# Key and value casts kept at their written places, and tile gaps that set moving and stationary addresses 416 bytes apart modulo 512

## The chip, the core and the metric

The kernel runs on one core of a Trainium2 chip. The metric is the time of one execution on the device in microseconds (us), lower is better. Beside it stands one execution taken by the hardware profiler; its records of engines, DMAs and waits are called the trace, and a summary of it is called the profile's page. PE is the matrix engine, PEld its weight loads, ACT, DVE and POOL are the scalar, vector and general engines, SP the engine that issues most DMAs.

## What is computed

One layer of an encoder for 256 positions of width 2048: several mixers side by side and an output projection, then cross attention to 256 memory rows, then a gated feed-forward part. Cut to the parts that the change touches:

```python
def cross_attention(h, mem_n, w_q, w_kv, w_o):          # 4 heads of 512
    q = (h @ w_q).reshape(bsz, seq, XA_HEADS, XA_HD)
    k, v = jnp.split(mem_n @ w_kv, 2, axis=-1)
...
    s = jnp.einsum('bshd,bmhd->bhsm', q, k).astype(jnp.float32) * XA_HD ** -0.5
    p = jax.nn.softmax(s, axis=-1).astype(v.dtype)
    o = jnp.einsum('bhsm,bmhd->bshd', p, v).reshape(bsz, seq, D_MODEL)
    return o @ w_o

def swiglu(h, w_gate_up, w_down):                       # inner width 5632
    gate, up = jnp.split(h @ w_gate_up, 2, axis=-1)
    return (jax.nn.silu(gate) * up) @ w_down
...
    x = x + mix @ w_out[l]
    x = x + cross_attention(rms_norm(x, norm_g[l, 1]), mem_n, w_xq[l], w_xkv[l], w_xo[l])
    x = x + swiglu(rms_norm(x, norm_g[l, 2]), w_gate_up[l], w_down[l])
```

## The kernel before, in words

**Precision.** Every large product is made from numbers split in a high part (rounded to the matrix engine's fast 4-byte type) and a low part (the rest). A tile of activations is 128 x 512: 256 columns of high parts and 256 of low parts. `mm` (L262 to L272) makes one 128 x 128 weight block's share of a product from two matmuls: the high weights `wh` with all 512 columns (L269), and the low weights `wl` with the 256 high columns (L270). The two together are called a pair here. The weights are the stationary operand, the activations the moving one. (`narrow` columns, L266 and L267, use three matmuls of 256 columns.) `gemm_rows` (L321 to L323) has them the other way round.

**Weights.** `Stream` reads all weights in the order of use. `_half` loads 2048 columns by SP's queue into one of three `raw` buffers and casts them, 1024 columns at a time, on ACT (`wh`, L89) and subtracts on DVE (`wl`, L90). Such a half feeds eight pairs. `wh` and `wl` have three buffers each, and a fourth while the pool `wx` is open (the mixers and the attention, up to nearly the end of `w_xo`).

**Stages, in the order of PE.** The keys and values of the memory (`w_xkv`), written to DRAM; the mixers (`w_in`); the output projection `out_proj` (`w_out`, 16 columns of 16 blocks); the attention (`w_xq` head by head, for each head the scores, softmax and values in `head`; then `w_xo`); `mlp` (`w_gate_up`, then `w_down`, 16 columns of 44 blocks: 8 tiles `act4` to `act11` and 36 tiles `f0` to `f35`). In `out_proj` the first four columns are made together, in three parts of the 16 blocks, because the mixers' results come late; each of the four columns has its own PSUM bank of the four in pool `psG`. The fifth column needs the first one's bank again. A finished bank is evacuated by `merge` (L274 to L278): ACT copies half of it (L276), DVE adds the other half (L178).

**Keys and values.** `load_kv`, a generator that runs beside the matmuls, brings the 16 key pieces and 16 value pieces back from DRAM. `fetch` (L580) issues a DMA on POOL's queue into one of five buffers `mr`. A key piece is cast on ACT (L186) and subtracted on DVE (L178, called by `split`), a value piece likewise (L194 and L178, called by `split2`); then the next piece is fetched.

**What sets the order.** Each engine runs its instructions in one fixed order. The Python program writes them in some order: `Background` polls the generators between matmuls, by planned costs. After that a scheduler of the framework orders each engine's instructions again by its own estimate of when they are ready, within their dependencies. In the kernel before, 16 of the 32 casts and subtractions of keys and values (those of heads 0 and 1) stand in ACT's and DVE's order in the first part of `out_proj`, far ahead of the place where the program writes them, which is among the first heads' query products. On ACT they stand between the casts of weights: four key casts, a value cast, a weight cast, two value casts, a weight cast, and so on, 16 in all, and 15 of them stand ahead of the copy (L276) that evacuates `out_proj`'s first column. The other 16 stand in four bursts of four among the products of heads 2 and 3.

**Addresses.** The tile pools give every tile one start address per partition. Those that matter here, modulo 512:

| tile | role | before | after |
|---|---|---|---|
| `act0` to `act23` | moving (stationary in `gemm_rows`) | 128 | 128 |
| `wh`, `wl` | stationary | 224 | 224 |
| `f0` to `f35` | moving, `w_down` | 224 | 128 |
| `oex0` to `oex3` | moving, `w_xo` | 224 | 128 |
| `kt` | moving, scores | 256 | 256 |
| `q` | stationary, scores | 256 | 352 |
| `pt` | moving, values | 224 | 128 |
| `vh`, `vl` | stationary, values | 256 | 224 |

Weight blocks are 512 bytes wide, so all blocks of a half have one place modulo 512, and so do the high and low halves of a moving tile.

Of the kernel before, what the change touches and what calls it, by code (L numbers as in the profile page):

```python
# [13 lines left out]
F32 = mybir.dt.float32  # L14
F32R = mybir.dt.float32r
# [7 lines left out]
P = 128  # L23
# [126 lines left out]
class Block:  # L150
# [42 lines left out]
    def split2(self, hi, lo, src):  # L193
        self.nc.scalar.copy(hi, src)  # L194
        self.tt(lo, src, hi.bitcast(F32), ALU.subtract)

    def sumsq(self, acc, src, first):
        if first:
            self.nc.scalar.activation(acc, src, AF.Square)
        else:  # L200
            s = self.tmp()
            self.nc.scalar.activation(s, src, AF.Square)
            self.tt(acc, acc, s, ALU.add)
# [343 lines left out]
    def attention(self):  # L547
        tc, nc, act, st = self.tc, self.nc, self.act, self.st
        with tc.tile_pool(name="atp", bufs=1) as atp, tc.tile_pool(name="kp", bufs=1) as kp, \
                tc.tile_pool(name="mp", bufs=5) as mp:  # L550
            oex = [atp.tile([P, 512], F32R, name=f"oex{i}") for i in range(4)]
            pt = [atp.tile([P, 512], F32R, name=f"pt{i}") for i in range(2)]
            qs = atp.tile([P, 2], F32, name="qs")
            o = act[0:8] + oex + act[8:12]
            slot = lambda name, n: kp.tile([P, 512], F32R, name=name, tag=name, bufs=n)
            kv = [([], [], []) for _ in range(4)]

            def ev_q(q, p):
                q.append(slot("q", 8))
                self.split(q[-1], self.merge(p))  # L560

            def scales():

                col = self.rstd_begin([[self.acc]], D)
                nc.vector.tensor_scalar(out=qs, in0=col, scalar1=512 ** -0.5, scalar2=None, op0=ALU.mult)
                yield

            heads = []

            def load_kv():  # L570

                todo = [(hd, what, i) for hd in range(4) for what in range(2) for i in range(4)]
                parts = []

                def fetch():
                    if len(parts) < len(todo):
                        hd, what, i = todo[len(parts)]
                        m = mp.tile([P, R], F32, name="mr", tag="mr")
                        o = (4 * hd + i) * R
                        nc.gpsimd.dma_start(m, (self.vd if what else self.kd)[:, o:o + R])  # L580
                        parts.append(m)

                for _ in range(5):
                    fetch()
                yield 4
                for n, (hd, what, i) in enumerate(todo):
                    while hd > len(heads) + 1:
                        yield
                    if what == 0:
                        kv[hd][0].append(slot("kt", 8))  # L590
                        self.split(kv[hd][0][-1], parts[n])
                    else:
                        if i % 2 == 0:
                            kv[hd][1].append(slot("vh", 4))
                            kv[hd][2].append(slot("vl", 4))
                        c = slice(i % 2 * R, i % 2 * R + R)
                        self.split2(kv[hd][1][-1][:, c], kv[hd][2][-1][:, c], parts[n])
                    fetch()
                    yield 1.0

            def scores(hd, q):
                while len(kv[hd][2]) < 2:
                    yield
                yield
                yield from self.head(q, *kv[hd], pt, o[4 * hd:4 * hd + 4], qs)
                heads.append(hd)

            lp = [list(range(8)), list(range(8, 16))]
            self.bg.add(scales())
            self.bg.add(load_kv())  # L610
            gens = []
            for hd in range(4):
                q = []
                if hd > 1:
                    self.bg.drain(gens[hd - 2], True)
                self.gemm("w_xq", [(4 * hd + i) * P for i in range(4)], self.h2, lambda i, p: ev_q(q, p), first=(4, lp),
                          before=lambda n: n and hd == 0 and self.bg.drain(self.late))
                gens.append(self.bg.add(scores(hd, q)))
            h3 = self.h3 = act[12:24] + act[0:4]

            def ev_o(i, p):
                self.residual(i, p, V_NG + 32 + i, h3[i] if i < 12 else None)
                if i == 12:
                    st.extra = None

            self.gemm("w_xo", [i * P for i in range(16)], o,
                      ev_o,
                      first=(4, [list(range(12)), list(range(12, 16))]), before=lambda n: n == 1 and self.bg.drain())
            self.bg.add(self.rest(h3, 12, V_NG + 32))
# [41 lines left out]
    def mlp(self):  # L671
        tc, nc, act = self.tc, self.nc, self.act
        with tc.tile_pool(name="fp", bufs=1) as fp:
            f = act[4:12] + [fp.tile([P, 512], F32R, name=f"f{i}") for i in range(36)]
            box = {}

            def ev(i, p):
                u = self.merge(p)
                self.tt(u, u, box["rs"], ALU.mult)
                if i % 2 == 0:  # L680
                    nc.scalar.activation(u, u, AF.Silu)
                    box["g"] = u
                else:
                    self.tt(u, u, box["g"], ALU.mult)
                    self.split(f[i // 2], u)

            cols = []
            for j in range(FT):
                cols += [j * P, DFF + j * P]
            self.bg.add(self.rstd_later(self.acc, D, box))  # L690
            self.gemm("w_gate_up", cols, self.h3, ev, first=(4, [list(range(12)), list(range(12, 16))]),
                      before=lambda n: n and self.bg.drain())
            warm = self.tmp()[:, 0:1]
            nc.scalar.activation(warm, self.ones[:, 0:1], AF.Sqrt)
            last = self.tmp()

            def ev_down(i, p):
                x = self.resk(i)
                self.tt(x, x, p[:, 0:R] if i == 15 else self.merge(p), ALU.add)
                sq = last if i == 15 else self.acc if i == 0 else self.tmp()  # L700
                nc.scalar.activation(sq, x, AF.Square)
                if 0 < i < 15:
                    self.tt(self.acc, self.acc, sq, ALU.add)
                nc.scalar.activation(x, x, AF.Copy, scale=self.gvec(V_FG, i))

            self.gemm("w_down", [i * P for i in range(16)], f, ev_down,
                      first=(4, [list(range(40)), list(range(40, 44))]), narrow_last=True)

            p = self.bank()[:, 0:R]
            for i, a in enumerate((self.acc, last)):  # L710
                nc.tensor.matmul(p, self.ones, a, start=i == 0, stop=i == 1)
            v, y, a, rs = (self.tmp() for _ in range(4))
            nc.vector.tensor_scalar(out=v, in0=p, scalar1=1.0 / D, scalar2=EPS, op0=ALU.mult, op1=ALU.add)
            nc.scalar.activation(a, v, AF.Sqrt)
            nc.vector.reciprocal(y, a)
            self.stt(a, y, -0.5, y, ALU.mult, ALU.mult)
            self.tt(a, a, v, ALU.mult)
            self.stt(p, a, 1.5, y, ALU.add, ALU.mult)
            nc.scalar.copy(rs, p)
            for i in range(0, KT, 2):  # L720
                x = self.res[i // 4][:, i % 4:i % 4 + 2, :]
                if i in POOLS:
                    nc.gpsimd.tensor_tensor(out=x, in0=x, in1=rs.unsqueeze(1).to_broadcast([P, 2, R]), op=ALU.mult)
                else:
                    self.tt(x, x, p.unsqueeze(1).to_broadcast([P, 2, R]), ALU.mult)
                (nc.scalar if i % 4 else nc.sync).dma_start(self.t["out"][:, i * R:(i + 2) * R], x.rearrange("p k r -> p (k r)"))
# [513 lines left out]
```

## Time and profile before

| | |
|---|---|
| median of 3 runs (lowest to highest) | 1527.2 us (1527.15 to 1528.36) |
| the profiled execution: its own time, its span | 1526.68 us, 1524.6 us |
| PE busy | 1502.2 us, 99% of the span, 8788 matmuls |
| PEld busy | 1311.2 us, 86% |
| DVE busy | 995.5 us, 65% |
| ACT busy | 787.3 us, 52% |
| chain that ended last | PE 96% |
| granted clock of TensorE over the span | 0.995 |

Matmuls are pipelined: the start of one overlaps the end of the one before, so their busy times add to more than the time that passes, and what one costs is read from the distance between starts. "Idle before" names what an engine waited for.

### The profile page before, as it was taken

How to read it: one execution, taken by the hardware profiler on the slowest of the kernel's cores; microseconds unless marked ns; L12 is line 12 of the kernel's file. 1: busy time of each engine (PE TensorE's matmuls, PEld its weight loads, DVE VectorE, ACT ScalarE, POOL GpSimd, SP SyncE). 2: the span in 40 equal slices, each digit the busy share in tenths (PEclk: the TensorE clock that was granted, in tenths of full speed). 3: DMA queues.
4: the chain of work that ended last, by engine and by line, in shares of the span. 5: the costliest groups of instructions: out<-in, count | busy, mean ns of one | idle time of the engine just before them, and what ended most of it. 6: DMA issues, size and time to landing. Idle time of an engine off the chain costs nothing.

```text
span 1524.6 us, 22257 instructions
## 1 busy us (share of the span) xinstructions
PE 1502.2 (99%) x8788; PEld 1311.2 (86%) x8788; DVE 995.5 (65%) x1532; ACT 787.3 (52%) x1238; POOL 40.0 (3%) x76
## 2 busy tenths in 40 slices
PE   8999999999999999999999999999999999999996
PEld 7887788889999788888888888888888888888885
DVE  6676668678667766867766666666666664555454
ACT  6664555557445655656554444444444444444442
POOL 0100100000002000100000000000000000000000
PEclk9999999999999999999999999999999999999998
DMA  9965554354346555544545555555555555555552
GB/s 353 343 239 190 198 193 166 139 195 159 139 167 241 195 190 182 177 149 166 194 166 193 189 185 185 189 192 194 193 193 186 186 186 190 192 192 180 183 191 83
DMA packets 48808, 290.53 MB, mean 191 GB/s; under 512 B 6173, under 2 KB 7486, under 8 KB 17088
## 3 DMA queue, kind: packets, MB, share of 16 engines
q1 hardware_dynamic: 44912, 279.59, 51.5%
q0 software_dynamic: 3072, 8.39, 1.6%
q8 instruction: 69, 1.13, 0.3%
q10 hardware_dynamic: 720, 1.13, 0.2%
q14 instruction: 35, 0.29, 0.0%
HBM read 282.80 MB, written 6.29 MB: 190 GB/s over the span
## 4 chain that ended last, share of the span: by engine, by line
PE 96%; DVE 1%; DMA 1%; issue 1%; ACT 0%; SPq 0%; POOL 0%; DVEq 0%; POOLq 0%; ACTq 0%
PE pg L269 49%; PE pg L270 28%; PE pg L266 3%; PE pg L267 3%; PE pg L321 3%; PE pg L323 2%; PE pg L322 2%; PE pm L269 1%; PE pm L796 1%; DMA mr<-values 1%; PE pm L664 1%; PE pm L270 0%; PE pm L637 0%; DMA raw<-in_W 0%; DVE wl L90 0%
## 5 line engine op out<-in xcount | busy, mean ns | idle before, releaser
L269 PE MATMUL pg<-act,wh 128*128 128x512 f32 x2680 | 939.7, 394 | 8.3 <-DVE act L182 4.5
L90 DVE TENSOR_TENSOR wl<-raw,wh 128x1024 fp32r<-128x1024 f32 (+1 forms) x507 | 617.0, 1218 | 425.9 <-ACT wh L89 423.6
L270 PE MATMUL pg<-act,wl 128*128 128x256 f32 x3008 | 842.5, 281 | 0.0
L89 ACT CAST wh<-raw 128x1024 fp32r<-128x1024 f32 (+1 forms) x507 | 529.5, 1046 | 589.5 <-PE pg L269 333.4
L269 PEld LDWEIGHTS pg<-act,wh 128*128 128x128 f32 x2680 | 504.7, 188 | 120.7 <-ACT wh L89 4.5
L270 PEld LDWEIGHTS pg<-act,wl 128*128 128x128 f32 x3008 | 566.9, 189 | 2.6 <-issue 2.0
L269 PE MATMUL pg<-f,wh 128*128 128x512 f32 x540 | 191.3, 398 | 0.0
L270 PE MATMUL pg<-f,wl 128*128 128x256 f32 x576 | 161.8, 281 | 0.0
L269 PEld LDWEIGHTS pg<-f,wh 128*128 128x128 f32 x540 | 101.5, 188 | 25.2
L270 PEld LDWEIGHTS pg<-f,wl 128*128 128x128 f32 x576 | 108.8, 189 | 0.0
L266 PE MATMUL pg<-act,wh 128*128 128x256 f32 x328 | 94.8, 289 | 0.0
L267 PE MATMUL pg<-act,wh 128*128 128x256 f32 x328 | 92.1, 281 | 0.0
L178 DVE TENSOR_TENSOR tmp<-pg,tmp 128x256 f32<-128x256 f32 x183 | 76.2, 417 | 5.7 <-ACT tmp L276 5.0
L276 ACT COPY tmp<-pg 128x256 f32<-128x256 f32 x179 | 65.0, 364 | 14.6 <-PE pg L270 14.5
L321 PE MATMUL pg<-wh,act 128*128 128x512 f32 x160 | 66.4, 415 | 0.0
L323 PE MATMUL pg<-wh,act 128*128 128x512 f32 x160 | 63.3, 395 | 0.0
L322 PE MATMUL pg<-wl,act 128*128 128x512 f32 x160 | 62.9, 393 | 0.0
L266 PEld LDWEIGHTS pg<-act,wh 128*128 128x128 f32 x328 | 61.9, 189 | 0.7
L267 PEld LDWEIGHTS pg<-act,wh 128*128 128x128 f32 x328 | 61.9, 189 | 0.3
L178 DVE TENSOR_TENSOR tmp<-tmp,rs 128x256 f32<-128x256 f32 x88 | 37.3, 425 | 2.9
L321 PEld LDWEIGHTS pg<-wh,act 128*128 128x128 f32 x160 | 30.0, 188 | 10.4 <-issue 2.9
L322 PEld LDWEIGHTS pg<-wl,act 128*128 128x128 f32 x160 | 30.1, 188 | 7.5 <-issue 1.0
(233 smaller groups left out, 985.1 us busy)
## 6 DMA issues: line engine op xcount, KB each, us to landing
raw<-in_W SPq DMA_DIRECT2D x247, 1024.0 KB, 4.8
raw<-in_W SPq DMA_DIRECT2D x9, 512.0 KB, 7.3
res<-in_xT SPq DMA_DIRECT2D x8, 512.0 KB, 5.6
k<-in_mem SPq DMA_DIRECT2D x8, 256.0 KB, 9.0
k<-in_x SPq DMA_DIRECT2D x8, 256.0 KB, 8.2
keys<-tmp POOLq DMA_DIRECT2D x16, 128.0 KB, 5.7
values<-tmp POOLq DMA_DIRECT2D x16, 128.0 KB, 2.4
mr<-keys POOLq DMA_DIRECT2D x16, 128.0 KB, 3.5
```

Source lines behind the costliest of these rows:

```text
L89: nc.scalar.copy(wh[:, a:b], r[:, a:b])
L90: nc.vector.tensor_tensor(out=wl[:, a:b], in0=r[:, a:b], in1=wh[:, a:b].bitcast(F32), op=ALU.subtract)
L178: self.nc.vector.tensor_tensor(out=out, in0=a, in1=b, op=op)
L266: self.nc.tensor.matmul(p[:, 0:R], wh, slot[:, 0:R], start=start, stop=False)
L267: self.nc.tensor.matmul(p[:, 0:R], wh, slot[:, R:512], start=False, stop=False)
L269: self.nc.tensor.matmul(p[:, :], wh, slot[:, :], start=start, stop=False)
L270: self.nc.tensor.matmul(p[:, 0:R], wl, slot[:, 0:R], start=False, stop=stop)
L276: self.nc.scalar.copy(t, p[:, R:512])
L321: nc.tensor.matmul(ps[r][:, :], hi, wh, start=k == 0, stop=False)
L322: nc.tensor.matmul(ps[r][:, :], hi, wl, start=False, stop=False)
L323: nc.tensor.matmul(ps[r][:, :], lo, wh, start=False, stop=k == nk - 1)
L664: nc.tensor.matmul(p[:, :], vh[m][:, s], pt[m][:, :], start=m == 0, stop=False)
```

## The change

Two things are done. `keep_place` adds, for each cast and subtraction that `load_kv` writes, an ordering edge without a semaphore to the instruction that was written before it on the same engine, so that the scheduler cannot put it ahead of that one. The computation and the number of compute instructions of each engine are the same. In the built program the 32 casts now stand one, two or at times three between neighbouring weight casts, from the first query products of head 0 to the values of head 3, and the orders of ACT, DVE and PE up to `out_proj` are otherwise as they were. During the attention some instructions change places: the transposes of the softmax (L656 before) stand one to ten pairs earlier or within a pair of where they stood, and the matmuls on the values move by a few pairs.

`gap` takes a tile that nothing uses, to shift what follows in its pool. With it, and with pools of their own for `q` and for `vh`, `vl` and a wider `qs`, the addresses become those of the last column of the table above.

```diff
+    def gap(self, pool, n):
+
+        pool.tile([P, n // 4], F32, name=f"gap{next(self.kept)}")
+
+    def keep_place(self, mark):
+
+        ins = self.nc.cur_bb.bb.instructions
+        for n in range(mark, len(ins)):
+            for j in range(n - 1, -1, -1):
+                if ins[j].engine == ins[n].engine:
+                    self.tc.add_manual_dep(ins[n], ins[j].name, mybir.DependencyInfo(
+                        mybir.DependencyClass.NoSync, mybir.DependencyReason.DATA), reason="order")
+                    break
...
     def attention(self):
         tc, nc, act, st = self.tc, self.nc, self.act, self.st
         with tc.tile_pool(name="atp", bufs=1) as atp, tc.tile_pool(name="kp", bufs=1) as kp, \
+                tc.tile_pool(name="qp", bufs=1) as qp, tc.tile_pool(name="vp", bufs=1) as vp, \
                 tc.tile_pool(name="mp", bufs=5) as mp:
+            self.gap(atp, 416)
+            self.gap(qp, 96)
+            self.gap(vp, 384)
             oex = [atp.tile([P, 512], F32R, name=f"oex{i}") for i in range(4)]
             pt = [atp.tile([P, 512], F32R, name=f"pt{i}") for i in range(2)]
-            qs = atp.tile([P, 2], F32, name="qs")
+            qs = atp.tile([P, 32], F32, name="qs")[:, 0:2]
             o = act[0:8] + oex + act[8:12]
-            slot = lambda name, n: kp.tile([P, 512], F32R, name=name, tag=name, bufs=n)
+            slot = lambda name, n: dict(kt=kp, q=qp).get(name, vp).tile([P, 512], F32R, name=name, tag=name, bufs=n)
...
                     while hd > len(heads) + 1:
                         yield
+                    mark = len(tc.nc.cur_bb.bb.instructions)
                     if what == 0:
                         kv[hd][0].append(slot("kt", 8))
                         self.split(kv[hd][0][-1], parts[n])
...
                         self.split2(kv[hd][1][-1][:, c], kv[hd][2][-1][:, c], parts[n])
+                    self.keep_place(mark)
                     fetch()
...
         with tc.tile_pool(name="fp", bufs=1) as fp:
+            self.gap(fp, 416)
             f = act[4:12] + [fp.tile([P, 512], F32R, name=f"f{i}") for i in range(36)]
```

## The prediction

> **What bounds the kernel now.** The page's first part and its chain of waits say the same: the matrix engine.
>
> ```profile
> PE 1502.2 (99%) x8788; PEld 1311.2 (86%) x8788; DVE 995.5 (65%) x1532; ACT 787.3 (52%) x1238; POOL 40.0 (3%) x76
> PE 96%; DVE 1%; DMA 1%; issue 1%; ACT 0%; SPq 0%; POOL 0%; DVEq 0%; POOLq 0%; ACTq 0%
> ```
>
> So a gain needs one of two things: a place where PE stands still, or matmuls that follow each other more slowly than they could. I next asked for all that PE waited for, over the whole span:
>
> ```profile
> PE pg L269 <- DVE act L182: 4.5, 1, 4.5
> PE pg L269 <- DVE tmp L178: 3.7, 1, 3.7
> PE pm L711 <- ACT tmp L701: 0.5, 1, 0.5
> PE pm L269 <- ACT wh L89: 0.5, 1, 0.5
> ```
>
> The first is at the kernel's start and the third at its end; the change touches neither. The second is a wait of 3.7 us for a bank of PSUM. The timeline from 494.9 us shows it:
>
> ```profile
> 494.92 0.28 PE L270 MATMUL pg<-act,wl 128*128 128x256 f32 x1
> 495.94 0.40 ACT L194 CAST vh<-mr 128x256 fp32r<-128x256 f32 x1 [3.02 <-DMA mr<-values]
> 496.25 1.04 ACT L89 CAST wh<-raw 128x1024 fp32r<-128x1024 f32 x1
> ...
> 497.20 0.70 ACT L194 CAST vh<-mr 128x256 fp32r<-128x256 f32 x2
> ...
> 497.81 0.36 ACT L276 COPY tmp<-pg 128x256 f32<-128x256 f32 x1
> ...
> 498.47 0.42 DVE L178 TENSOR_TENSOR tmp<-pg,tmp 128x256 f32<-128x256 f32 x1
> ...
> 498.94 0.79 PE L269 MATMUL pg<-act,wh 128*128 128x512 f32 x1 [3.73 <-DVE tmp L178]
> ```
>
> PE's last matmul of the first four columns of `w_out` starts at 494.92; the fifth column starts at 498.94, when DVE has emptied the first bank. That bank was complete 12 pairs before the end of the group, about 494.9 - 12 x 0.347 = 490.8. The copy that empties it is the row at 497.81: on ACT it stood behind casts of keys and values, one of which sat 3.02 us for its DMA. ACT's waits from 479 to 500 us hold 9.4 us for `mr` in all (5.1 on values, 4.3 on keys).
>
> The table of stretches gives the clock after that:
>
> ```profile
> 498.94:504.22 5.28, 5.28 (x16) 0.50 0.76 273
> 504.67:510.20 5.53, 5.53 (x34) 1.00 0.56 188
> 800.00:1280.00 480.00, 480.00 (x2769) 422.49 (x2769) 309.00 (x429) 232.15 (x344) 0.00 (x0) 1.00 0.53 189
> ```
>
> The last three numbers of a row are granted clock, DMA share and GB/s: the clock is 0.50 until 504.2, and 1.00 again in the second row. The third is the steady rate of `w_gate_up` with `act` tiles: 480 us for 2769 matmuls or 1384.5 pairs, 346.7 ns a pair.
>
> Last, the rate of `w_down`. One column runs through `act4` to `act11` and `f0` to `f35`, with the same weights, at clock 1.00:
>
> ```profile
> 1354.51 0.39 PE L269 MATMUL pg<-act,wh 128*128 128x512 f32 x1
> ...
> 1357.28 0.40 PE L269 MATMUL pg<-f,wh 128*128 128x512 f32 x1
> ...
> 1369.98 0.39 PE L269 MATMUL pg<-act,wh 128*128 128x512 f32 x1
> ```
>
> These rows are starts: 8 pairs on `act` take 2.77 us, 346 ns each; the 36 on `f` take 12.70 us, 353 ns each. By the trace's exact starts a column has 2.774 and 12.706 us, 346.8 and 352.9 ns, in each of four columns looked at. Nothing waits there. By the table of addresses `act` starts 416 bytes past the weights modulo 512, `f` 0 bytes past.
>
> **Part 1: the held casts.** Removed from ACT ahead of the copy at 497.81: 15 casts and their DMA waits. Then ACT's order there is weight casts and the copy alone. Would the copy be in time? With the same spacing as the weight casts before the casts of keys (476.01, 478.54: one per 8 pairs, 2.77 us), the weight cast ahead of it stands near 490, the copy at about 491 when the bank is complete, DVE's addition ends about 0.8 us later (0.36 and 0.42), near 492, 3 us before PE needs the bank. The residual's rows of x, which DVE needs next, were issued by SP at 470.4 and 474.2 and land in 4.5 us. The weights of the fifth column were cast and subtracted by 493.9 even before. So I see nothing that is late next there. The price: from the start of PE's last row ahead of the wait (494.69) to the first of full speed again (504.67) are 10 pairs in 9.98 us; at 346.7 ns they take 3.47. **Removed: 6.5 us**, 3.7 of it the wait, the rest the half clock.
>
> On the clock the row stands first: a stop of 4.0 us between the starts, then 0.50 for 5.5 us. The Trainium skill (TensorE: Matmul & The Clock Gate, Part 1) says that an idle window of about 3.4 us brings the half clock. The trace agrees, and by that rule a shorter stop left over would cost its own length only.
>
> Added: nothing in number. The 16 casts and 16 subtractions of heads 0 and 1 move to the products of `w_xq`, the first eight to about 575 to 593 us, and the other 16 are spread out. In place, 32 of them cost 32 x 0.31 = 10 us of ACT and 32 x 0.34 = 11 us of DVE over some 70 us. DVE has room: from 580 to 600 us it is busy 11.4 of 20, from 600 to 660 us 14.6 to 16.2. What waits behind a cast on ACT is the next weight cast, and behind a subtraction the next weight subtraction. The cover is their lead: in the trace each `wl` half is done 5.6 to 9.4 us ahead of its first use between 580 and 700 us. One cast with its subtraction is 0.7 us; two or three together use a third of the lead. Should the cover go, each further cast costs PE its 0.31 us.
>
> What has no such lead is the softmax of each head: ten operations on DVE and ACT between PE's scores and PE's transposes. In the new order the transposes of heads 0 and 1 stand about 1 to 5 pairs earlier. Going through the new orders with the old rows' durations: head 0 loses four subtractions of 0.33 us inside its chain and is ready at about 3.0 and 3.7 us after the scores against transposes at 3.5 and 3.9; head 1 has its second half ready near 4.4 against 4.1, so 0.3 us of PE; its values wait another 0.25 for a `pt` subtraction with a key's ahead of it; head 2 as before; head 3 has both exponentials side by side and is ready sooner. I take **+0.4 us**. Bounds: -1.0, all stops of 60 to 150 ns by this stage's transposes gone, and +3.7, one stop like that of 494.9 without its clock.
>
> POOL's queue: 32 fetches of 0.55 us in the same order, each released by the subtraction five pieces earlier. A fetch lands 3.6 us after its issue (5.2 at most); with casts some 2 us apart, five buffers are 10 us of room. The bursts of before were 0.31 us apart, and that outran them. SP's queue is not passed by anything.
>
> **Part 2: the gaps.** No instruction is added. `w_down` has 15 full columns with 36 `f` pairs: 15 x (12.706 - 36 x 0.3468) = 15 x 0.22 = 3.3 us. The sixteenth is narrow: its rows are at 283 ns against 281 to 289, nothing. `oex` in `w_xo`: by starts, 14 pairs of 361 ns and 40 of 349: 0.3 us. Scores (32 pairs) and values (32 pairs) differ by 2 or 3 ns from the others: 0.1 us. **Removed: 3.7 us.** Since `f` after has the very addresses modulo 512 that `act` has, the rate is taken from the same stage, not from a theory; whether the distance or the start modulo 64 (`f` 32, `act` 0) does it makes no difference here. Bounds: 0 and 4.0.
>
> Against this speaks a rule of the Trainium skill (TensorE: Matmul & The Clock Gate, step ① of Part 2): weights and moving operand have independent read ports, and loading the next weights takes nothing from the running matmul. By it the gaps give nothing, the second rival below; 353 against 346 ns in one column do not look like it.
>
> **Sum**, from the profiled execution: 1526.68 - 6.5 - 3.7 + 0.4 = 1516.9; that execution is 0.5 under the median of the runs, 1527.2, so 1517.4 by that. I take **1517.0**, between them; its own range is 1515 to 1518.7. A measurement of this kernel tells 0.2% (3.05 us) from no change.
>
> **The rivals.**
> 1. *A wait takes the stop's place* at 494.9 (the residual's addition, a late weight half) or in a softmax chain: 1 to 4 us come back. For it: DVE in its order has the weight subtractions of 1.22 us ahead of the merge and in the chains. Against it: a margin of 3 us and leads of 5.6 us. Time 1518.7 to 1521. Chance 0.10.
> 2. *The gaps give nothing*: weight loads and moving reads don't disturb each other, and `f` is slow for another reason than its address modulo 512 (which part of the memory it lies in, or what is written beside it): -6.5 + 0.4 from both bases, 1520.6 to 1521.1. Chance 0.05. (The Trainium skill's rule of part 2, in TensorE: Matmul & The Clock Gate, ends here.)
> 3. *The held casts do to the attention what the free ones did to `out_proj`*: a cast at ACT's head waits for its DMA (3.0 us in the row at 495.94), banks fill, PE stops, the clock halves, 6.5 us each time. One stop leaves 1523.5, two 1530.0, about today's time; with three, one for each of heads 1 to 3, whose keys are fetched on demand, 1536.5, slower. It decides from two stops on, that is if casts come faster than five in 5.2 us. The order says one to three per weight half of 2.77 us. Chance 0.05, of that 0.02 for one stop, 0.01 for two, 0.02 for three.
> 4. *It doesn't do what it says*: not here; orders and addresses of the built program show both.
>
> **Chances.** Forecast 0.80, rivals 0.10, 0.05, 0.05. Faster by over 0.2% (below 1524.1): 0.80 + 0.10 + 0.05 + 0.02 = 0.97, of which I take 0.01 off for what I do not see: 0.96. Within 0.2%: 0.02. Slower: 0.02. The range takes the forecast's own and both ends of rivals 1 and 2: 1514.8 to 1521.0.
>
> **What would show it.** PE's list of waits without the row of 3.7 us; no stretch of clock 0.50 near 500 us; in `w_down` 36 `f` pairs of a column in 12.5 us; `wl` leads in the attention still above 3 us; no PE wait on L178 or L186 between 570 and 700 us. It is wrong if ACT waits for `mr` by more than 2 us in the attention, or if `f` stays at 353 ns.

## The result, and the profile after

The median is 1515.77 us (six runs, 1515.14 to 1516.05) against 1527.49 us (six runs, 1526.0 to 1528.36): a ratio of 0.9923 with a 95% interval of 0.9911 to 0.9934, or 10 to 14 us faster. The forecast was 1517.0, with a range of 1514.8 to 1521.0. The profiled execution took 1515.95 us with a span of 1513.9, against 1526.68 and 1524.6. So the medians are 11.7 us apart and the two profiled executions 10.7; where the time went is read from the executions.

The page of the changed kernel (engines; chain of waits), and all that PE waited for:

```profile
PE 1495.1 (99%) x8788; PEld 1308.1 (86%) x8788; DVE 996.2 (66%) x1532; ACT 786.4 (52%) x1238; POOL 40.1 (3%) x76
PE 99%; DVE 0%; DMA 0%; ACT 0%; SPq 0%; issue 0%; DVEq 0%
```

```profile
PE pg L283 <- DVE act L182: 4.6, 1, 4.6
PE pm L732 <- ACT tmp L722: 0.5, 1, 0.5
PE pm L283 <- ACT wh L89: 0.5, 1, 0.5
```

The counts of instructions are those of before. The wait of 3.7 us is gone from the list, and the chain now is PE at 99%, where before 1% each of DMA, DVE and "issue" stood in it. The same stretches as before show the clock (third number from the right):

```profile
494.70:498.94 4.24, 4.24 (x26) 1.00 0.38 147
498.94:504.22 5.28, 5.28 (x33) 1.00 0.58 200
504.67:510.20 5.53, 5.53 (x34) 1.00 0.50 185
```

From 498.94 to 504.22 PE starts 33 matmuls where it started 16. And this is why the stop is gone, on ACT:

```profile
489.50 1.05 ACT L89 CAST wh<-raw 128x1024 fp32r<-128x1024 f32 x1 [1.72 <-PE pg L283]
491.01 0.37 ACT L290 COPY tmp<-pg 128x256 f32<-128x256 f32 x1 [0.45 <-PE pg L284]
492.28 1.05 ACT L89 CAST wh<-raw 128x1024 fp32r<-128x1024 f32 x1 [0.90 <-PE pg L283]
```

The copy that empties the first bank (L290, which was L276) starts at 491.01 in place of 497.81. In front of it ACT waits for PE, no longer for a DMA. The addition on DVE that ends the emptying follows at 491.73:

```profile
491.73 0.42 DVE L178 TENSOR_TENSOR tmp<-pg,tmp 128x256 f32<-128x256 f32 x1
```

A column of `w_down` in the timeline:

```profile
1346.15 0.39 PE L283 MATMUL pg<-act,wh 128*128 128x512 f32 x1
...
1348.92 0.39 PE L283 MATMUL pg<-f,wh 128*128 128x512 f32 x1
...
1361.40 0.39 PE L283 MATMUL pg<-act,wh 128*128 128x512 f32 x1
```

The 8 `act` pairs take 2.77 us as before, the 36 `f` pairs 12.48 in place of 12.70: 346.7 ns a pair, the same as `act`.

Where the time went is seen best by one number along the kernel: how much earlier each matmul starts than the same one in the profiled execution of before. The order of PE is nearly the same in all kernels here, so the n-th matmul stands for a place. (Starts counted from the first matmul, which is 4.5 us after the span's start; microseconds; minus is later.)

| n-th matmul, its start before | 2762 (460.6) | 3362 (567.6) | 4164 (707.2) | 4566 (777.4) | 7267 (1245.6) | 8767 (1502.9) |
|---|---|---|---|---|---|---|
| place | ahead of `w_out` | end of `w_out` | attention's end | end of `w_xo` | end of `w_gate_up` | end of `w_down` |
| changed kernel | 0.09 | 6.61 | 6.52 | 6.98 | 6.98 | 10.69 |
| e1, held casts alone | 0.19 | 6.70 | 6.30 | 6.32 | 6.32 | 6.32 |
| e2, gaps alone | 0.03 | -1.09 | -0.79 | -0.34 | -0.35 | 3.37 |
| e6, casts not held, without DMA | 0.36 | 6.87 | 7.15 | 7.61 | 7.61 | 11.32 |
| e7, held from the ninth | -1.61 | 4.90 | 4.79 | 5.24 | 5.23 | 8.95 |
| e8, held from the fourteenth | 0.27 | 0.06 | -0.02 | 0.42 | 0.42 | 4.13 |

For the changed kernel: 6.5 us in `w_out`, next to nothing (-0.09) in the attention, 0.46 in `w_xo`, nothing in `w_gate_up`, 3.7 in `w_down`. The first column is how far executions differ before the changed code begins.

### The profile page after: what moved, and what is told of

The parts are those of the page before. It is cut to its first block, busy times and chain, and to the rows that moved or that the text cites. A ratio compares the mean times of both kernels' runs of the same rounds, so it can differ in the third digit from the quotient of the medians.

```text
span 1513.9 us, 22263 instructions
## 1 busy us (share of the span) xinstructions
PE 1495.1 (99%) x8788; PEld 1308.1 (86%) x8788; DVE 996.2 (66%) x1532; ACT 786.4 (52%) x1238; POOL 40.1 (3%) x76
## 4 chain that ended last, share of the span: by engine, by line
PE 99%; DVE 0%; DMA 0%; ACT 0%; SPq 0%; issue 0%; DVEq 0%
PE pg L283 50%; PE pg L284 28%; PE pg L280 3%; PE pg L281 3%; PE pg L335 3%; PE pg L337 2%; PE pg L336 2%; PE pm L283 1%; PE pm L817 1%; PE pm L684 1%; PE pm L284 0%; PE pm L657 0%; DMA raw<-in_W 0%; PE pm L260 0%; PE pm L658 0%; PE pm L229 0%
## 5 line engine op out<-in xcount | busy, mean ns | idle before, releaser
L283 PE MATMUL pg<-f,wh 128*128 128x512 f32 x540 | 187.9, 392 | 0.0
L290 ACT COPY tmp<-pg 128x256 f32<-128x256 f32 x179 | 65.0, 364 | 14.8 <-PE pg L284 14.7
L335 PEld LDWEIGHTS pg<-wh,act 128*128 128x128 f32 x160 | 30.0, 188 | 10.4 <-issue 2.9
L337 PEld LDWEIGHTS pg<-wh,act 128*128 128x128 f32 x160 | 30.1, 188 | 7.5
```

What stands on the lines that cost most here:

```text
L283: self.nc.tensor.matmul(p[:, :], wh, slot[:, :], start=start, stop=False)
L290: self.nc.scalar.copy(t, p[:, R:512])
L335: nc.tensor.matmul(ps[r][:, :], hi, wh, start=k == 0, stop=False)
L337: nc.tensor.matmul(ps[r][:, :], lo, wh, start=False, stop=k == nk - 1)
```

## The experiments

My theory was two independent effects. ACT's queue was blocked at its head by casts that waited for DMA, which kept a PSUM bank full and stopped PE; and a pair of matmuls takes longer or shorter by how its moving tile lies to the weights. The rivals are named with each run.

### e1 and e2: each half alone

e1 is the kernel before with `keep_place` alone:

```diff
+                    mark = len(tc.nc.cur_bb.bb.instructions)
                     if what == 0:
...
+                    self.keep_place(mark)
                     fetch()
```

> The held casts alone, with the addresses of the kernel before. My theory: the stop at 494.9 us and the half clock behind it go, 6.6 us, and the attention stays as it was: 1527.5 - 6.6 = 1520.9 us. The 36 f pairs of a w_down column still take 12.70 us. Rival (part of the gain of the change comes from both together, or the attention gained from the addresses): 1519 or less, or 1522 and more.

Measured: 1520.62 us, ratio 0.9961 (0.9947 to 0.9976). e2 is the changed kernel without it:

```diff
-                    self.keep_place(mark)
                     fetch()
```

> The addresses of the changed kernel alone, with the order of instructions of the kernel before. My theory: 3.8 us from w_down and 0.3 from w_xo: 1527.5 - 4.1 = 1523.4 us, with the wait of 3.7 us and the clock of 0.50 near 500 us unchanged. Rival (the stop takes in what the addresses gave elsewhere): 1525 or more.

Measured: 1522.9 us, ratio 0.9975 (0.9965 to 0.9985). In the same series the kernel before had a median of 1526.15 us (13 runs), and not the 1527.5 from which both expectations start. So by the medians e1 gains 5.5 us for the 6.6 expected, and e2 3.3 for 4.1; the times themselves are as the theory had them. By the table e1 gains 6.5 us in `w_out`, loses 0.4 in the attention, and gains nothing after; e2 gains 0.30 in the attention, 0.45 in `w_xo` and 3.7 in `w_down`. The two together, stage by stage, are the changed kernel within 0.1 us but for one number, so there are two effects and neither needs the other: e2 loses 1.1 us in `w_out`, where it has the order of before. Its timeline shows the old stop, longer:

```profile
497.59 0.40 ACT L194 CAST vh<-mr 128x256 fp32r<-128x256 f32 x1 [3.19 <-DMA mr<-values]
...
499.46 0.36 ACT L290 COPY tmp<-pg 128x256 f32<-128x256 f32 x1
...
500.59 0.79 PE L283 MATMUL pg<-act,wh 128*128 128x512 f32 x1 [5.36 <-DVE tmp L178]
```

The same program order stopped PE for 3.7 us in one profiled execution and 5.4 in another. So the stop's size varies from one execution to the next. That fits the spread of the runs (2.4 us before, 2.6 us for e2, 0.9 for the changed kernel, 0.7 for e1), though I show it on two traces only. That it is the DMAs' times that vary is likely, and not shown.

### e6, e7 and e8: what in the free casts stops PE

e6 leaves the casts free and takes the loads away:

```diff
-                        m = mp.tile([P, R], F32, name="mr", tag="mr")
-                        o = (4 * hd + i) * R
-                        nc.gpsimd.dma_start(m, (self.vd if what else self.kd)[:, o:o + R])
-                        parts.append(m)
+                        parts.append(self.rsm)
...
-                    self.keep_place(mark)
```

> Leaves out the loads of keys and values back from DRAM: all 32 pieces are cast from one tile that is there from the start, so the attention computes on wrong keys and values. Addresses of the changed kernel, casts not held: the scheduler again puts 16 of them into out_proj, ahead of the copy of its first bank. Theory: what blocked ACT was the wait for the DMA, 9.4 us of it, and not the casts' own 16 x 0.31 = 5 us: no stop of PE near 495 us, no half clock, 1515 to 1516 us. Rival: the casts' own time on ACT and DVE delays the copy too: a stop of 1 to 4 us stays, 1518 to 1522 us.

Measured: 1515.03 us in one run, and no wait of PE but the three of the changed kernel. On ACT:

```profile
480.03 1.32 ACT L186 CAST kt<-krs 128x256 fp32r<-128x256 f32 x4
481.26 1.04 ACT L89 CAST wh<-raw 128x1024 fp32r<-128x1024 f32 x1
482.21 1.32 ACT L194 CAST vh<-krs 128x256 fp32r<-128x256 f32 x4
...
490.74 0.37 ACT L290 COPY tmp<-pg 128x256 f32<-128x256 f32 x1 [0.45 <-PE pg L284]
```

All 16 casts stand ahead of the copy, four in 1.32 us, and the copy starts at 490.74, as early as in the changed kernel. So the early place of the casts costs nothing by itself; the wait for their DMA at the head of an in-order queue does. (Without loads the scheduler placed them up to three weight casts earlier, so the order is not quite that of before: there three weight casts stand between the last of the 16 and the copy.)

e7 and e8 hold only the later casts:

```diff
-                    self.keep_place(mark)
+                    if n >= 8:
+                        self.keep_place(mark)
```

> The changed kernel with the first eight casts (head 0) not held: they go back to out_proj, ahead of the copy. Theory: in the trace of before ACT was through with eight by 489.7, the bank is complete at 490.8, two weight casts of 1.05 us follow: the copy is at about 492, no stop, and the softmax of head 0 has less beside it: 1515.5 to 1516. Rival (any of the free casts ahead of the copy costs): a stop of 1 to 4 us, 1517 to 1522.

> The same with the first 13 casts free: the thirteenth, the first value of head 1, is the one that waited 3.02 us for its DMA in the trace of before. Theory: ACT is held until about 496, then a weight cast, and the copy comes near 497.3: a stop of about 3 us. Whether the clock falls to 0.50 behind a stop of that length is open: if it does, 1521 to 1522 us, if not, 1519. Rival: without the last three casts the fetches come sooner and nothing stops, 1516.

Measured: e7 1517.7 us, e8 (13 in place of 8) 1522.71 us, one run each. e7 missed its range by its start: 1.6 us late by the table's first column, before anything that the edit touches. (Its matmuls start at half rate until 13.05 us, those of before until 9.49.) From there to the end of `w_out` it gains 6.5 us, as the changed kernel does, with eight casts free and ACT waiting 5.6 us for `mr`: those waits end before the bank is complete. With 13 free the thirteenth is the one that blocks:

```profile
496.34 0.40 ACT L194 CAST vh<-mr 128x256 fp32r<-128x256 f32 x1 [3.14 <-DMA mr<-values]
496.65 1.04 ACT L89 CAST wh<-raw 128x1024 fp32r<-128x1024 f32 x1
...
497.60 0.36 ACT L290 COPY tmp<-pg 128x256 f32<-128x256 f32 x1
497.72 1.22 DVE L90 TENSOR_TENSOR wl<-raw,wh 128x1024 fp32r<-128x1024 f32 x1 [0.52 <-ACT wh L89]
...
498.86 0.41 DVE L178 TENSOR_TENSOR tmp<-pg,tmp 128x256 f32<-128x256 f32 x1
...
499.33 0.79 PE L283 MATMUL pg<-act,wh 128*128 128x512 f32 x1 [4.24 <-DVE tmp L178]
```

The copy came when expected (497.60 for 497.3), but the stop is 4.2 us and not 3: the copy is not the last thing that PE waits for. DVE's addition comes 0.9 us after the copy's end, behind the weight subtraction of 1.22 us that stands ahead of it on DVE. In the kernel before the addition at 498.47 stood behind such a row too, and I had read past it:

```profile
497.32 1.23 DVE L90 TENSOR_TENSOR wl<-raw,wh 128x1024 fp32r<-128x1024 f32 x1 [0.52 <-ACT wh L89]
```

The clock in e8 then is 0.50 from 498 to 504, and the whole 6.5 us of the stop are back (0.27 to 0.06 in the table).

### e3, e4, e5, e9 and e10: which distances are good

e3 spreads the `f` tiles over all multiples of 32 bytes; e4 does the same with the weights 32 bytes further on:

```diff
-            f = act[4:12] + [fp.tile([P, 512], F32R, name=f"f{i}") for i in range(36)]
+            f = act[4:12]
+            for i in range(36):
+                f.append(fp.tile([P, 512], F32R, name=f"f{i}"))
+                self.gap(fp, 32)
```

> The changed kernel with 32 bytes between any two f tiles, so that the 36 tiles start at 416, 448, 480, 0, 32, ... bytes past the weights modulo 512, twice round. Read: the time of a pair by distance. Theory A, the distance to the weights counts: about 353 ns at 0 and perhaps near it, 346.7 at the other distances. Rival B, the start modulo 64 counts: 353 and 346.7 ns in turn. Rival C, the place in the memory counted: 346.7 ns at all. If some distance is below 346.7, a better kernel exists.

> As e3_sweep, with the weight tiles (and all behind them) 32 bytes further on, and the f tiles at the same starts modulo 512 as there: each tile's distance to the weights is 32 less. act tiles are at distance 384. Theory A: the curve over the distance is that of e3_sweep, so the slow tiles are one further on in the row (f4 and f20 in place of f3 and f19), and gate_up runs at what e3_sweep shows for 384. Rival B: the same tiles as in e3_sweep are slow, since their own starts are the same, and gate_up stays at 346.7 ns.

Measured: 1518.43 and 1530.24 us, one run each. The median time of a pair over all full columns, by the distance of its moving tile to the weights modulo 512:

| distance | 0 | 32 | 64 | 96 | 128 | 160 | 192 | 224 |
|---|---|---|---|---|---|---|---|---|
| e3, ns | 350 | 351 | 351 | 354 | 348 | 347 | 359 | 346 |
| e4, ns | 349 | 351 | 350 | 355 | 348 | 347 | 359 | 347 |
| **distance** | **256** | **288** | **320** | **352** | **384** | **416** | **448** | **480** |
| e3, ns | 350 | 351 | 351 | 354 | 348 | 347 | 359 | 347 |
| e4, ns | 350 | 351 | 351 | 355 | 347 | 347 | 359 | 348 |

By these medians the two kernels agree at each distance, although a given distance has another tile, start and place in memory in each: in the second half of a column the tiles that take 359 ns are `f17`, `f25` and `f33` in e3 and `f18`, `f26` and `f34` in e4, one further on, as the weights are. In the first half of e3's columns they do not all agree: `f1`, at 448, takes 347 ns there, and `f2`, at 480, 362. So what stands ahead of a tile counts too. Tiles that start at a multiple of 64 are among the fast and among the slow. Rivals B (start modulo 64) and C (place in memory) fall. The numbers for 0 to 224 repeat at 256 to 480: here it counts modulo 256. What theory A said of the other distances, 346.7 ns at all but 0, was wrong: most are slower.

224 and 480 looked as good as 416. e5 moves the weights so that `act` is at 224, and half of `f` at 480:

```diff
+        pool("gw", 1).tile([P, 48], F32, name="gapw")
         rawp = pool("rawp", 3)
...
-            self.gap(fp, 416)
+            self.gap(fp, 480)
...
+                if i == 18:
+                    self.gap(fp, 448)
```

> The changed kernel with the weight tiles 192 bytes further on: the act tiles are then 224 bytes past the weights, the tiles f0 to f17 480 bytes past them, f18 to f35 416. In the two sweeps distances 224 and 480 had the pairs nearest to 416's, 345.7 to 351 ns with mixed neighbours. If only the distance counts and it repeats after 256 bytes, act at 224 and f at 480 run at the same rate; if that is 345.7 ns, gate_up (1408 pairs) gains 1.4 us and w_down 0.3: 1514 us. If 416 is as good as any: within 1 us of 1515.8. If a uniform row at 224 or 480 behaves like that of 0 (353 ns instead of the 349 of the sweep): 1520 to 1525.

Measured: 1533.86 us, ratio 1.0043 (1.0026 to 1.006), slower than before. The last of the three expectations held, and cost more than its 1520 to 1525. The same stretch, nearly all of it `w_gate_up`, in e5 and then in the kernel before:

```profile
800.00:1280.00 480.00, 480.00 (x2719) 1.00 0.52 186
```

```profile
800.00:1280.00 480.00, 480.00 (x2769) 1.00 0.53 189
```

2719 matmuls against 2769 in 480 us, at the same clock and with no wait: by starts, 353.3 ns a pair at 224, 346.7 at 416. In `w_down` the 18 tiles at 480 took 353.3, the 18 at 416 346.7. So a sweep in which every neighbour has another distance does not tell what a distance costs among its like. e9 and e10 therefore have groups of six with one distance each:

```diff
-            self.gap(fp, 416)
...
+                if i % 6 == 0:
+                    self.gap(fp, 32)
```

> The changed kernel with the 36 f tiles in six groups of six, 32, 64, 96, 128, 160 and 192 bytes past the weights modulo 512, to see each distance among its like (in the sweeps every neighbour had another one). Theory: the distance counts modulo 256, so 160 runs as 416 does, 346.7 ns, and 128 as 384, 351; 32, 64, 96 and 192 at 349 to 359 as in the sweeps. Rival (it counts modulo 512): 160 differs from 346.7. If one is below 346.7, a better kernel exists.

e10 gets its steps of 4 bytes as slices of larger tiles:

```diff
+            for g, (skip, o) in enumerate(((0, 4), (480, 6), (480, 7), (0, 1), (480, 2), (480, 4))):
+                if skip:
+                    self.gap(fp, skip)
+                big = fp.tile([P, 3080], F32R, name=f"f{g}")
+                f += [big[:, o + 512 * k:o + 512 * k + 512] for k in range(6)]
```

> The changed kernel with the f tiles in six groups of six, 400, 408, 412, 420, 424 and 432 bytes past the weights (starts that are not multiples of 32, as slices of larger tiles). Theory: lines of 16 or 32 bytes are what meets, so 420 and 424 run as 416 does, 346.7 ns, and 400 to 412 as 384, 351. Rival: every step of 4 bytes counts, and some of them lie under 346.7 ns, or 416 alone is good.

Measured: 1518.45 and 1517.74 us, one run each. Mean pair of a long row of one distance where a kernel has one, else of the inner four of a group of six:

| distance | 0 | 32 | 64 | 96 | 128 | 160 | 192 | 224, 480 | 384 | 400 | 408 | 412 | 416 | 420 | 424 | 432 |
|---|---|---|---|---|---|---|---|---|---|---|---|---|---|---|---|---|
| ns | 353.0 | 346.8 | 349.4 | 351.2 | 351.0 | 347.2 | 352.4 | 353.3 | 351.1 | 349.6 | 355.0 | 346.5 | 346.7 | 353.4 | 346.6 | 350.2 |
| from | before | e9 | e9 | e9 | e9 | e9 | e9 | e5 | e4 | e10 | e10 | e10 | all | e10 | e10 | e10 |

160 runs nearly as 416 does (347.2 for 346.7) and 128 as 384: modulo 256 once more. But neighbours 4 bytes apart differ, 412, 416 and 424 fast, 420 slow, so lines of 16 or 32 bytes do not explain it. Nothing is below 346.5 by more than these means can tell, so 416 is one of several best distances and no faster kernel follows from the sweep. Four pairs in a group are few: 64 to 192, 400, 408 and 432 may not have settled. (For 192 a row of 16 pairs, at the end of the first four columns, settles at 353.3.)

## Why the prediction was right

**The stop (predicted -6.5, measured -6.5).** Chain, place and price held: 0.09 to 6.61 in the table, 6.5 in e1, and 6.5 back in e8. Nothing took its place: the copy came at 491.01 for "about 491", DVE's addition at 491.73. That the DMA waits block and not the casts' own time was right (e6). What the chain left out is that the wait runs through a weight subtraction on DVE too, which stood only under the first rival, and that the stop's length differs from run to run.

**The attention (predicted +0.4 for the casts).** e1 shows 0.4, so the size was right, but the place was wrong. Heads 0 to 2 cost 0.05 together (6.71 at matmul 3462, 6.66 at 3962); head 3, which I thought would be ready sooner, costs 0.36 (6.30 at 4070). There the scores wait for the last `q` subtraction, 0.29 us in e1: the new order puts a weight subtraction ahead of it that stood behind it before. In the changed kernel's trace:

```profile
673.93 1.22 DVE L90 TENSOR_TENSOR wl<-raw,wh 128x1024 fp32r<-128x1024 f32 x1 [0.93 <-ACT wh L89]
675.07 0.42 DVE L178 TENSOR_TENSOR q<-tmp,q 128x256 fp32r<-128x256 f32 x1
```

The transposes of both halves stand side by side and wait 0.23 us for the second half, about as long as they did before (0.24). So 0.4 was the right size for a wrong reason, which is luck. The loss does not show in the changed kernel, since the addresses give 0.3 back in the same stage. ACT waited for no `mr` at all in the attention, and the lead of `wl` stayed at 5.6 us or more from 580 to 700, as the prediction asked.

**The gaps (predicted -3.7, measured -4.4).** `w_down` 3.7 for 3.3: the full columns gave the 3.4 us that 540 x (353.0 - 346.7) makes, and the narrow column another 0.3, which I had put at nothing. I had compared busy times there (283 against 281 to 289 ns); the distances of starts say 360 ns a triple before and 352 after. `w_xo` gave 0.45 for 0.3, the attention 0.30 for 0.1. These three make up nearly all of the 0.8 us by which the sum, 9.8, fell short of the 10.6 of the table.

**The rivals.** No wait took the stop's place in the changed kernel. That the gaps give nothing is refuted by e2: 346.7 against 353.0 ns by address alone, at one clock and without waits. This speaks against the rule of the Trainium skill (TensorE: Matmul & The Clock Gate, step ① of Part 2) that loading the next weights takes nothing from the running matmul, as far as it is taken to mean that addresses cannot matter. The measurement decides on the time; that it is the weight loads that the moving reads meet is not shown. The slower outcome did not come near: the casts came some two per weight half, and five buffers were enough.

**The clock.** The prediction said of a shorter stop that it would cost its own length only. The traces do not bear that out. The three stops seen in `w_out`, 3.7, 4.2 and 5.4 us, all halved the clock, and it fell while PE still stood. In the kernel before, PE's last matmul ended at 495.20 by the profile, and the clock (third number from the right) was 0.50 from 497.6 on:

```profile
495.20:497.55 2.35, 0.00 (x1) 1.00 0.62 237
497.65:498.94 1.29, 0.00 (x1) 0.50 0.31 102
```

That is 2.4 us after the last matmul; in e8 it was 2.3 us and in e2 2.9. In each of the three it stayed at 0.50 for 6.8 us, so what was left of it when PE started again was 5.5, 4.9 and 4.3 us. No run had a shorter stop in `w_out`, so from what length on the clock falls stays open.

Open too: why some distances are fast. The runs show that the distance of moving and stationary operand decides, with what stands ahead in the row, and not the start or the place; they do not show what meets in the memory. The casts on ACT and subtractions on DVE do not set it: they come once per eight pairs, while the times of the pairs on `f` before repeat after three.

## What to carry to other kernels

Where an engine runs in order, ask of every instruction that a scheduler pulled forward what it waits for, and what stands behind it: here early casts were free as long as their waits ended before the bank was complete (e6, e7), and cost 6.5 us when one sat on a DMA until the bank's copy was late. A matrix engine at 99% can still have slow and fast pairs: compare distances between starts for each tile, at one clock, and if two groups with equal work differ, compare their addresses. Try a distance in long rows of its own, not in a mixed sweep: 224 bytes looked best in the sweep and made the kernel 6 us slower than before.

## What the runs showed of the hardware that I had not expected

A pair (512 and 256 moving columns) settles at 346.7 ns at its best distances and near 353.3 at bad ones. Distances 4 bytes apart can lie on either side (416 and 420), and in the sweeps the times repeat after 256 bytes. Between single pairs the times alternate in fixed patterns: on `f` before, 349, 350 and 361 ns over and over. A stop of PE of 3.7 us cost 6.5, because the clock fell to 0.50 within it and stayed there for over 5 us behind it.
